# Order of the first stage of a hybrid encoder layer: written order on all engines, earlier scaling of query and key banks, stores from the wide weight tile

## The chip, the cores and the metric

The kernel runs on one core of a Trainium2 chip. The metric is the device time of one execution in microseconds (us); lower is better. Three runs of the kernel before gave 2736.58, 2729.5 and 2735.8 us, median 2735.8 us. One further execution was profiled; all rows below come from it.

## The reference

One layer on a sequence of 2048 tokens of width 1024, cut to what matters:

```python
mod = silu(c) @ w_ada + b_ada                     # six vectors: shift, scale, gate, twice
h = rmsnorm(x, g_norm1) * (1 + sc1) + sh1
q_sb, k_sb, v_sb, q_ca, k_ca, v_ca = split(h @ w_in)
o_sb = stick_breaking_attention(q_sb, k_sb, v_sb) # 8 heads
q_ca, k_ca = rmsnorm(q_ca, g_q), rmsnorm(k_ca, g_k)   # per head of 64
o_ca = chunked_relpos_attention(q_ca, k_ca, v_ca, rel_bias)  # 8 heads
x = x + gt1 * (concat(o_sb, o_ca) @ w_o)
x = x + gt2 * (relu(h2 @ w1) ** 2 @ w2)           # h2: the second norm of x
```

The matrices are fp32. The kernel splits each operand into a high and a low part (`split`: ScalarE copies the high part, a subtraction gives the low one) and multiplies three times, high by high, high by low and low by high (`mm3`). Every product is thus three matmuls.

## The kernel before, in words

The kernel has three stages: the input projection (this change), the two attentions with their output projection, and the MLP. Only the first stage is touched.

**Tiles and jobs.** The sequence has four blocks of 512 tokens, numbered 3 to 0. Weights come in pieces: pieces 0 to 3 are halves of the query and key columns of the first head group (256 columns each, 1 MB raw), 4 and 10 are the values of the two groups, 6 and 8 the queries and keys of the second group (512 columns, two raw tiles of 1 MB). A job is (f, piece, block). A small piece gives two PSUM banks, a large one four; a bank is 8 steps of `mm3`, 24 matmuls. The first three pieces (2, 0, 1) of block 3 are multiplied together while the data arrive; their weights are split into one tile `wide` (pieces 0 and 1) and four tiles of the weight pool (piece 2). Then the list `jobs` runs: 58 banks up to the last job and 4 more in the last one, 62 in all.

**Pools.** A raw weight tile comes from a ring of three (`load_raws`), a split weight from a pool of nine (`weight_parts`, two rows of 512 fp32 each). A split weight that the later stage needs is stored to scratch memory `scr_w`; its buffer is free for the next piece when TensorE has read it and the store has landed. `wide` and the normalised blocks 2 and 0 share one buffer (tag `hp`). PSUM has six banks for this stage, used in turn. Staged results (`st`, `sv`, `wow`) share three buffers.

**Second group.** For pieces 6 and 8 each bank of raw queries or keys needs a norm per head: ScalarE squares it (`csq`), VectorE reduces it (`cv`), GpSimd takes the inverse root in five small operations (`cy`), VectorE scales the bank into `qh` (`scale`). After the fourth bank TensorE transposes the four `qh` into `px` banks (`turn`), two at a time, which are then scaled, split and stored. `later` holds `scale` and `turn` back by a number of banks (a tick follows each bank): 2 for `scale`, 3 and 4 for the two halves of `turn`.

**Block norms.** `start_norm` squares and sums the eight tiles of a block, `norm_rstd` and `norm_spread` (banks `pva` and `pra`) make the inverse root and spread it, VectorE multiplies the tiles by it, and `end_norm` scales, shifts and splits them into the block's `ht`, eight tiles one after the other on ScalarE and VectorE. `hook` says at which bank this happens.

**Side work.** `ada` loads a row group of `w_ada` and, two ticks later, takes a dot product of it on VectorE (`CUSTOM_DVE_ANT_0`, printed as ISA in the order). `prepare_bias` and `prepare_wo` bring the bias and the output weights into scratch memory. A credit per bank in `run_job` paces them.

**Order.** `Ordered` wraps an engine so that its instructions keep the order in which the program is written. TensorE has this throughout. The other engines and the DMA queue of SyncE have it for the first three pieces and from job 7 on; for the jobs ahead of it (`n < ORDERED`) a list scheduler chose their order. In either case the order is fixed when the kernel is built, and each engine takes its list strictly in turn.

Of the kernel before, what the change touches and what calls it, by code (L numbers as in the profile page):

```python
# [18 lines left out]
P = 128  # L19
# [6 lines left out]
TB = 512  # L26
# [53 lines left out]
def encoder_kernel(ctx, tc, xT, c, g1, g2, w_in, w_rest, gqk, bias, w_o, w1, w2, w_ada, b_ada, out):  # L80
# [161 lines left out]
    if True:  # L242
# [48 lines left out]

        def weight_parts(key, m):

            f, p = key
            w = w_tile(f"{f}_{p}_{m}")
            wts.setdefault(key, []).append(w)
            if p < 4:
                src = raws[key, 0][:, 2 * m : 2 * m + 2, :]
                hi, lo = (w[:, l, :].rearrange("p (k c) -> p k c", c=CW) for l in range(2))
# [15 lines left out]

        def weight_of(key, k):
            if key[1] < 4:
                w = wts[key][k // 2]
                return [w[:, l, (k % 2) * CW : (k % 2 + 1) * CW] for l in range(2)]
            return wts[key][k][:, 0, :], wts[key][k][:, 1, :]  # L320
# [6 lines left out]

        staged = {}

        def half_tile(nm, n):  # L330

            if n % 2 == 0:
                staged[0] = stp.tile([P, 2, 2, TB], F32R, tag="st", name=f"st{nm}")
            return staged[0][:, n % 2]

        def project(key, tb, ht, last):
# [3 lines left out]
            if piece < 4:  # L340
                kind, hf = divmod(piece, 2)
                for n in range(2):
# [10 lines left out]
                    store_qk(kind, 0, ps, half_tile(f"{nm}_{n}", n), hf * 2 + n, tb)  # L353
# [4 lines left out]
            for tt in range(4):  # L358
# [4 lines left out]
                for k in range(KT):  # L363
                    mm3(ps, ht[k][:, 0, tl], ht[k][:, 1, tl], *weight_of(key, k), k == 0, k == KT - 1)
                    if last and tt == 3:
                        free[0] += 1
                        pump()
                if kind == 2:
# [28 lines left out]
                later.add(2, scale)  # L397
                if tt == 3:
                    def turn(n):
# [3 lines left out]
                        store_qk(kind, 1, pt, half_tile(f"{nm}_{n}", n), n, tb, gqk_s[:, kind : kind + 1])  # L403

                    for n in range(4):
                        later.add(3 + n // 2, lambda n=n: turn(n))
# [24 lines left out]
        xts, hts = {}, {}  # L431

# [72 lines left out]
        w2s = [w_tile(f"first_{m}").rearrange("p l (k c) -> p l k c", c=CW) for m in range(4)]  # L505
        pss = [pp.tile([P, TB], F32, tag="ps", name=f"pq{p}_3_{n}") for p in first for n in range(2)]

        def first_w(k):
            wr = wraw[k // 2][:, k % 2]
            split(wide[:, k, 0, :, :], wide[:, k, 1, :, :], wr[:, 0:2, :], pool)  # L510
            split(w2s[k // 2][:, 0, k % 2], w2s[k // 2][:, 1, k % 2], wr[:, 2, :], pool)
# [10 lines left out]
        for k in range(KT):  # L522
# [10 lines left out]
            if k + 4 < KT:  # L533
                first_x(k + 4)
            for m, p in enumerate(first):
                hi, lo = [w2s[k // 2][:, l, k % 2] if p == 2 else wide[:, k, l, p] for l in range(2)]
# [6 lines left out]
        act, dve, pool = nc.scalar, nc.vector, nc.gpsimd  # L543
        osp.dma_start(gcol[:, 1, :], g2)
        osp.dma_start(gqk_sb, gqk)
        dve.tensor_scalar_mul(gqk_s[:, 0:1], gqk_sb[:, 0:1], 0.125)
        dve.tensor_copy(gqk_s[:, 1:2], gqk_sb[:, 1:2])
        jobs = [(0, 3, 3), (0, 6, 3), (0, 6, 2), (2, 3, 2), (2, 2, 2), (2, 0, 2), (2, 1, 2)]
        jobs += [(0, p, t) for p in (8, 4, 10) for t in (3, 2)]
        jobs += [(1, p, t) for p, t in ((6, 1), (6, 0), (8, 1), (8, 0), (4, 1))]  # L550
        keys = list(dict.fromkeys((f, p) for f, p, _ in jobs))
        loads = [(key, m) for key in keys for m in range(1 if key[1] < 4 else 2)]
        count = {key: 4 if key[1] < 4 else KT for key in keys}

        def load_raws(*q):

            while loads and len(raws) - sum(len(wts.get(k, ())) >= (4 if k[1] < 4 else 4 * m + 4) for k, m in raws) < 3:
                load_raw(*loads.pop(0), *q)

        free[0] += 4  # L560
        load_raw(*loads.pop(0), osp)
        load_x(2, osp)
        load_raws(osp)
        for m in range(4):
            weight_parts((0, 3), m)
        for m, p in enumerate(first):
            for n in range(2):
                grp, hf = divmod(p, 2)
                store_qk(grp, 0, pss[2 * m + n], half_tile(f"f{p}_3_{n}", n), hf * 2 + n, 3)
# [6 lines left out]
        ORDERED = 7  # L576
        start_norm(2, 2, 2)

        def hook(job, n):

            if (job, n) == ((0, 6, 3), 2):
                norms.flush()
                end_norm(2, h_tile(2))
                load_x(1)
# [13 lines left out]
        def run_job(n):  # L598
            nonlocal credit, act, dve, pool, sp
# [10 lines left out]
            for b in range(2 if key[1] < 4 else 4):  # L610
# [5 lines left out]
                credit += 2.2 if n >= ORDERED else 3.0 * (key[1] in CAQK)  # L616
# [1037 lines left out]
```

## Time and profile before

| | |
|---|---|
| median of three runs | 2735.8 us |
| profiled execution | 2737.15 us |
| its span on the profiler's clock | 2735.4 us |
| first stage: start to the first score matmul `z` | 0 to 462.67 us |
| TensorE busy over the span | 96% |
| mean granted TensorE clock | 0.984 |

The profiled execution is 1.75 us longer than its span and 1.35 us above the median. In rows of a timeline the columns are start and length in us, engine, line, operation, out<-in and count; in brackets stands the idle time of the engine just before and what ended it. L42 is the line of the wrapper `Ordered`; rows with L147, L215 and the like are from the jobs that the scheduler ordered. Rows of waits give us in total, how often, and the longest. `PEclk` is the granted TensorE clock as a share of full speed.

### The profile page before, as it was taken

To read this page: it belongs to the slowest core of one execution; us is meant where nothing else is said; L and a number is where in the kernel's file an instruction comes from. 1 tells how busy PE (TensorE), PEld (TensorE's weight loads), DVE (VectorE), ACT (ScalarE), POOL (GpSimd) and SP (SyncE) were. 2 spreads that over 40 slices of the span, in tenths; PEclk is the share of its full clock that TensorE was granted. 3 is DMA by queue.
4 is the path that set the end of the run, shared out by engine and by line. 5 is a ranking of instruction groups with operands and counts; after the bars stand their busy time and mean duration, and the time that the engine had idled before them with its cause. 6 is when DMAs were issued, how large, how long until landed. Compare 5 with 4: busy or idle time off the path is not lost. (4 is left out here: it accounts for less than half of the span.)

```text
span 2735.4 us, 40253 instructions
## 1 busy us (share of the span) xinstructions
PE 2622.0 (96%) x12944; PEld 2175.4 (80%) x12944; DVE 1922.0 (70%) x3215; ACT 1527.2 (56%) x2966; POOL 997.4 (36%) x1244
## 2 busy tenths in 40 slices
PE   7989999899899999999998999999999999999999
PEld 5767777778778988878776788878888888888887
DVE  7625664788789988989856778877866656655565
ACT  6423443788678877878653444455644444544443
POOL 4422043566456656767533332302101232300000
PEclk9999999999999999999999999999999999999999
DMA  9697967878888688766776777796665434365574
GB/s 341 240 351 277 338 271 238 254 247 249 268 252 263 201 243 266 231 207 190 214 247 224 248 264 260 252 333 228 235 245 201 153 140 162 140 237 199 202 261 155
DMA packets 265333, 651.28 MB, mean 238 GB/s; under 512 B 29856, under 2 KB 65696, under 8 KB 254240
## 3 DMA queue, kind: packets, MB, share of 16 engines
q1 hardware_dynamic: 264336, 646.60, 69.4%
q10 hardware_dynamic: 784, 2.10, 0.3%
q8 instruction: 103, 1.69, 0.3%
q14 instruction: 110, 0.90, 0.1%
HBM read 457.21 MB, written 191.37 MB: 237 GB/s over the span
## 5 line engine op out<-in xcount | busy, mean ns | idle before, releaser
L42 PE MATMUL ps<-h,opw 128*128 128x512 f32 x2664 | 609.8, 391 | 6.3 <-DVE cx L42 6.0
L42 PE MATMUL ps<-oph,opv 128*128 128x512 f32 x2688 | 610.9, 390 | 0.0
L42 PEld LDWEIGHTS ps<-h,opw 128*128 128x128 f32 x2664 | 500.6, 188 | 114.9 <-DVE cx L42 9.1
L42 PEld LDWEIGHTS ps<-oph,opv 128*128 128x128 f32 x2688 | 504.8, 188 | 104.5
L42 POOL TENSOR_TENSOR b<-b,p 128x512 f32<-128x512 f32 (+1 forms) x320 | 359.7, 1124 | 198.8 <-DVE p L42 176.3
L42 DVE TENSOR_TENSOR wtl<-wt,wth 128x512 fp32r<-128x512 f32 (+3 forms) x544 | 290.3, 545 | 50.4 <-ACT wth L42 47.9
L42 ACT CAST wth<-wt 128x512 fp32r<-128x512 f32 (+3 forms) x544 | 257.5, 484 | 119.7 <-PE wt L42 104.4
L42 PE MATMUL pt<-w,ht 128*128 128x512 f32 x1248 | 301.0, 402 | 19.3 <-ACT w L147 8.1
L42 DVE TENSOR_TENSOR oph<-hw,oph 128x512 fp32r<-128x512 f32 x224 | 161.0, 719 | 212.6 <-ACT oph L42 212.6
L42 ACT CAST oph<-hw 128x512 fp32r<-128x512 f32 x224 | 139.3, 622 | 288.9 <-PE ps L42 271.1
L42 PEld LDWEIGHTS pt<-w,ht 128*128 128x128 f32 x1248 | 239.1, 193 | 73.7 <-issue 10.9
L42 DVE TENSOR_TENSOR_SCAN p<-z,p,zero 128x512 f32<-128x512 f32 x192 | 246.0, 1281 | 34.4 <-ACT z L42 28.9
L42 POOL TENSOR_TENSOR ts<-w 128x512 f32<-128x512 f32 x32 | 44.6, 1394 | 549.6 <-DMA w<-in_w_dram 492.5
L42 PE MATMUL acc<-wth,v 128*128 128x512 f32 (+3 forms) x544 | 223.2, 414 | 1.4 <-DMA v<-scr_v 1.4
L42 ACT ACTIVATE b<-z 128x512 f32<-128x512 f32 (+1 forms) x320 | 171.4, 536 | 64.1 <-PE z L42 47.3
L42 POOL TENSOR_TENSOR e<-e,cols 128x640 f32<-128x640 f32 (+4 forms) x128 | 142.9, 1120 | 148.0 <-DVE cols L42 84.5
L42 PE MATMUL z<-k,q 128*128 128x512 f32 (+3 forms) x640 | 186.2, 373 | 9.0 <-DVE p L42 7.0
L42 PE MATMUL acc<-wtl,v 128*128 128x512 f32 (+3 forms) x544 | 187.3, 351 | 0.0
L42 PE MATMUL wt<-ident,b 128*128 128x128 f32 x1088 | 173.3, 275 | 7.0 <-DVE cols L42 5.0
L42 DVE TENSOR_TENSOR opw<-w,opw 128x512 fp32r<-128x512 f32 x127 | 96.9, 764 | 116.4 <-ACT opw L42 116.3
L42 PE MATMUL po<-fx,ow 128*128 128x512 f32 x576 | 167.4, 406 | 4.7 <-DMA ow<-scr_wo 4.7
L42 ACT ACTIVATE z<-z 128x512 f32<-128x512 f32 (+1 forms) x320 | 170.6, 533 | 0.0
(223 smaller groups left out, 4330.5 us busy)
## 6 DMA issues: line engine op xcount, KB each, us to landing
hw<-scr_hid SPq DMA_DIRECT2D x112, 512.0 KB, 3.8
v<-scr_v SPq DMA_DIRECT2D x136, 256.0 KB, 3.8
k<-scr_k SPq DMA_DIRECT2D x268, 128.0 KB, 4.0
w<-in_w_dram SPq DMA_DIRECT2D x64, 512.0 KB, 5.1
hw<-scr_s SPq DMA_DIRECT2D x64, 512.0 KB, 4.6
q<-scr_q SPq DMA_DIRECT2D x124, 256.0 KB, 5.1
fw<-scr_w SPq DMA_DIRECT2D x28, 1024.0 KB, 6.7
wa<-in_w_ada_dram SPq DMA_DIRECT2D x48, 512.0 KB, 7.1
```

The costliest lines, as they stand in the source:

```text
L42: return lambda *x, **y: self.tc.keep_in_program_order(f(*x, **y))
```

## The change

Seven edits, all in the first stage:

1. All engines and the DMA queue keep written order throughout; the switch at job 7 is gone.
2. `scale` of a bank goes right behind the next bank's matmuls (`scale_last`), one tick earlier, and `turn` comes after 2 and 3 ticks in place of 3 and 4.
3. In `jobs`, piece 8 moves ahead of pieces 0 and 1 of block 2; piece 8 stood behind them.
4. Pieces 0 and 1 are stored to `scr_w` from `wide`, in two DMAs of 2 MB, at the second bank of the first job; only pieces 2 and 3 are stored from weight tiles. Those have a new layout (high and low side by side), so a store of one tile is one DMA of 512 KB in place of two of 256 KB.
5. The low parts of the small pieces are subtracted on VectorE, not on GpSimd.
6. Loads: the first raw weight and block 2 are asked for inside the loop of the first three pieces; block 1 and block 0 one bank later; the second gains `gcol` and `gqk` behind the first stores, and the two small operations on `gqk` one job later.
7. `start_norm` of block 0 waits 3 ticks for its second part in place of 2; the credit per bank is 1.9 for large pieces, 2.0 or 1.0 (times f) for small ones, in place of 3.0, 0 or 2.2.

```diff
-            split(hi, lo, src, pool if p < 4 else dve)
-            if f == 2:
-                for l, x in enumerate((hi, lo)):
-                    behind.add(2, lambda l=l, x=x: sp.dma_start(scr_w[p,][:, 2 * m : 2 * m + 2, l, :], x.bitcast(F32)))
+            split(hi, lo, src)
+            if f == 2 and p > 1:
+                behind.add(2, lambda: sp.dma_start(scr_w[p,][:, 2 * m : 2 * m + 2], four(w).bitcast(F32)))
...
+        def scale_last():
+            while scales:
+                scales.pop(0)()
...
+                scale_last()
...
-                later.add(2, scale)
+                scales.append(scale)
...
-                        later.add(3 + n // 2, lambda n=n: turn(n))
+                        later.add(2 + n // 2, lambda n=n: turn(n))
...
+        jobs = [(0, 3, 3), (0, 6, 3), (0, 6, 2), (2, 3, 2), (2, 2, 2), (0, 8, 3), (0, 8, 2), (2, 0, 2), (2, 1, 2)]
+        jobs += [(0, p, t) for p in (4, 10) for t in (3, 2)]
...
-        jobs = [(0, 3, 3), (0, 6, 3), (0, 6, 2), (2, 3, 2), (2, 2, 2), (2, 0, 2), (2, 1, 2)]
-        jobs += [(0, p, t) for p in (8, 4, 10) for t in (3, 2)]
...
+            if k == KT - 3:
+                load_raw(*loads.pop(0), osp)
+                load_x(2, osp)
+            if k == KT - 1:
+                for m in range(4):
+                    weight_parts((0, 3), m)
...
-        act, dve, pool = nc.scalar, nc.vector, nc.gpsimd
...
+            if (job, n) == ((0, 3, 3), 1):
+                dve.tensor_scalar_mul(gqk_s[:, 0:1], gqk_sb[:, 0:1], 0.125)
+                dve.tensor_copy(gqk_s[:, 1:2], gqk_sb[:, 1:2])
+                for p in range(2):
+                    sp.dma_start(scr_w[p,], wide[:, :, :, p, :].bitcast(F32))
...
+            if (job, n) == ((0, 10, 2), 1):
                 load_x(0)
-                behind.add(3, lambda: start_norm(0, 2, 1))
+                behind.add(2, lambda: start_norm(0, 3, 1))
...
-            if n == ORDERED:
-                act, dve, pool = (Ordered(tc, e) for e in (nc.scalar, nc.vector, nc.gpsimd))
-                sp = osp
...
-                credit += 2.2 if n >= ORDERED else 3.0 * (key[1] in CAQK)
+                credit += 1.9 if key[1] > 3 else 1.0 * key[0]
```

Three places show what moves. The first is TensorE at the transposes of the first group of queries (`px_6_3_0`, made of the four scaled banks `qh_6_3_0` to `qh_6_3_3` of job (0, 6, 3)). Before, they follow the second bank of the next job, `pt_6_2_1`:

```order
L42 MATMUL pt_6_2_1_1123<-w_6_6_811,ht_949 128x512 x3
L42 MATMUL pt_6_2_1_1123<-w_6_7_820,ht_949 128x512 x3
L42 MATMUL px_6_3_0_1163<-ident,qh_6_3_0_943 128x128
L42 MATMUL px_6_3_0_1163<-ident,qh_6_3_1_1029 128x128
L42 MATMUL px_6_3_0_1163<-ident,qh_6_3_2_1073 128x128
L42 MATMUL px_6_3_0_1163<-ident,qh_6_3_3_1117 128x128
```

With the change they follow its first bank, `pt_6_2_0`:

```order
L42 MATMUL pt_6_2_0_1058<-w_6_6_813,ht_949 128x512 x3
L42 MATMUL pt_6_2_0_1058<-w_6_7_822,ht_949 128x512 x3
L42 MATMUL px_6_3_0_1098<-ident,qh_6_3_0_920 128x128
L42 MATMUL px_6_3_0_1098<-ident,qh_6_3_1_999 128x128
L42 MATMUL px_6_3_0_1098<-ident,qh_6_3_2_1042 128x128
L42 MATMUL px_6_3_0_1098<-ident,qh_6_3_3_1083 128x128
```

They stand one bank of 24 matmuls earlier, and so they do for each of the eight groups of transposes.

The second place is VectorE at the same group, from the last low part of block 2 (`ht` from `xt_7`) to the last scaled bank. Before, the two reductions `cv` stand together and the two scalings together:

```order
L148 TENSOR_TENSOR ht_949<-xt_7_687,ht_949 128x512
L383 TENSOR_REDUCE cv_6_3_2_1017<-csq_6_3_2_1015 128x8
L392 TENSOR_TENSOR qh_6_3_1_1029<-pt_6_3_1_893,cy_6_3_1_923 128x512
L384 TENSOR_SCALAR cv_6_3_2_1017<-cv_6_3_2_1017 128x8
L383 TENSOR_REDUCE cv_6_3_3_1062<-csq_6_3_3_1060 128x8
L260 ISA wa_947,mod<-wa_947,cs,bcol 128x1024
L260 ISA mod 128x1
L384 TENSOR_SCALAR cv_6_3_3_1062<-cv_6_3_3_1062 128x8
L392 TENSOR_TENSOR qh_6_3_2_1073<-pt_6_3_2_990,cy_6_3_2_1020 128x512
L392 TENSOR_TENSOR qh_6_3_3_1117<-pt_6_3_3_1035,cy_6_3_3_1065 128x512
```

With the change each reduction waits behind the scaling of the bank before it, and two dot products (ISA) stand between:

```order
L42 TENSOR_TENSOR ht_949<-xt_7_620,ht_949 128x512
L42 TENSOR_TENSOR qh_6_3_1_999<-pt_6_3_1_895,cy_6_3_1_927 128x512
L42 TENSOR_REDUCE cv_6_3_2_1003<-csq_6_3_2_1001 128x8
L42 TENSOR_SCALAR cv_6_3_2_1003<-cv_6_3_2_1003 128x8
L42 ISA wa_891,mod<-wa_891,cs,bcol 128x1024
L42 ISA mod 128x1
L42 ISA wa_893,mod<-wa_893,cs,bcol 128x1024
L42 ISA mod 128x1
L42 TENSOR_TENSOR qh_6_3_2_1042<-pt_6_3_2_974,cy_6_3_2_1006 128x512
L42 TENSOR_REDUCE cv_6_3_3_1046<-csq_6_3_3_1044 128x8
L42 TENSOR_SCALAR cv_6_3_3_1046<-cv_6_3_3_1046 128x8
L42 TENSOR_TENSOR qh_6_3_3_1083<-pt_6_3_3_1017,cy_6_3_3_1049 128x512
```

The reduction of the fourth bank has moved behind the scaling of the third.

The third place is the DMA queue of SyncE at the last stored weight piece ahead of piece 8. Before, that is piece 1 (`scr_w_221`), whose eight stores of 256 KB stand between stores of queries:

```order
L215 DMA scr_q_2_2_86<-st_1_2_0_1608 128x1024
L306 DMA scr_w_221<-w_1_0_1542 128x2x256 x2
L306 DMA scr_w_221<-w_1_1_1545 128x2x256 x2
L306 DMA scr_w_221<-w_1_2_1548 128x2x256 x2
L306 DMA scr_w_221<-w_1_3_1551 128x2x256 x2
L215 DMA scr_q_2_3_87<-st_1_2_0_1608 128x1024
```

With the change it is piece 2 (`scr_w_222`), four stores of 512 KB behind loads and stores of the two jobs ahead:

```order
L42 DMA scr_k_2_3_119<-st_3_2_0_1320 128x2x512
L42 DMA scr_q_2_2_102<-st_6_2_2_1396 128x1024
L42 DMA scr_q_2_3_103<-st_6_2_2_1396 128x1024
L42 DMA wa_1408<-in_w_ada_dram 128x1024
L42 DMA wr_0_1410<-in_w_in_dram 128x2048
L42 DMA scr_k_2_0_116<-st_2_2_0_1437 128x2x512
L42 DMA scr_w_222<-w_2_0_1351 128x1024
L42 DMA scr_w_222<-w_2_1_1354 128x1024
L42 DMA scr_w_222<-w_2_2_1357 128x1024
L42 DMA scr_w_222<-w_2_3_1360 128x1024
```

The stores of pieces 0 and 1 no longer stand here; those of piece 2 are now the last that piece 8 waits for.

More of the change, by code (lines that the diff above doesn't have):

```diff
@@ L298, in weight_parts @@
                 src = raws[key, 0][:, 2 * m : 2 * m + 2, :]
-                hi, lo = (w[:, l, :].rearrange("p (k c) -> p k c", c=CW) for l in range(2))
+                hi, lo = (four(w)[:, :, l, :] for l in range(2))
             else:
@@ L431, in encoder_kernel, with load_raws @@
         xts, hts = {}, {}
+        jobs = [(0, 3, 3), (0, 6, 3), (0, 6, 2), (2, 3, 2), (2, 2, 2), (0, 8, 3), (0, 8, 2), (2, 0, 2), (2, 1, 2)]
+        jobs += [(0, p, t) for p in (4, 10) for t in (3, 2)]
+        jobs += [(1, p, t) for p, t in ((6, 1), (6, 0), (8, 1), (8, 0), (4, 1))]
+        keys = list(dict.fromkeys((f, p) for f, p, _ in jobs))
+        loads = [(key, m) for key in keys for m in range(1 if key[1] < 4 else 2)]
+        count = {key: 4 if key[1] < 4 else KT for key in keys}
+        def load_raws(*q):
+            while loads and len(raws) - sum(len(wts.get(k, ())) >= (4 if k[1] < 4 else 4 * m + 4) for k, m in raws) < 3:
+                load_raw(*loads.pop(0), *q)
         def load_x(tb, q=None):
@@ L542, in encoder_kernel @@
                     )
-        act, dve, pool = nc.scalar, nc.vector, nc.gpsimd
[L544 to L547, printed above, removed]
-        jobs = [(0, 3, 3), (0, 6, 3), (0, 6, 2), (2, 3, 2), (2, 2, 2), (2, 0, 2), (2, 1, 2)]
-        jobs += [(0, p, t) for p in (8, 4, 10) for t in (3, 2)]
[L550 to L558, printed above, removed]
-        free[0] += 4
[L561 to L565, printed above, removed]
+        free[0] += 4
+        sp = osp
+        load_raws()
         for m, p in enumerate(first):
@@ L583, in hook @@
                 end_norm(2, h_tile(2))
+            if (job, n) == ((0, 6, 2), 1):
                 load_x(1)
```

28 lines of the change are left out of this document (16 added, 12 removed).

## The prediction

> **What bounds the kernel now.** The page comes first, with the busy times and the largest group of the first stage:
>
> ```profile
> PE 2622.0 (96%) x12944; PEld 2175.4 (80%) x12944; DVE 1922.0 (70%) x3215; ACT 1527.2 (56%) x2966; POOL 997.4 (36%) x1244
> L42 PE MATMUL pt<-w,ht 128*128 128x512 f32 x1248 | 301.0, 402 | 19.3 <-ACT w L147 8.1
> ```
>
> TensorE is the bound, and the change adds and removes no matmul. So only TensorE's idle time in the first stage can change. The second row confirms the count of banks: 1248 matmuls are 52 banks of 24; with the ten banks of small pieces that makes 62. The waits of TensorE up to 520 us name what holds it (total, times, longest):
>
> ```profile
> PE pva L42 <- DVE nsaa L42: 17.7, 2, 12.5
> PE pt L42 <- ACT w L147: 8.1, 3, 7.1
> PE pt L42 <- DVE qh L42: 7.3, 2, 4.6
> PE pt L42 <- DVE qh L392: 2.9, 1, 2.9
> ```
>
> The 12.5 us is the kernel's start, already in written order and not touched. The others lie behind 59.79 us. TensorE's timeline shows where, and what follows each:
>
> ```profile
> 59.79 11.04 PE L42 MATMUL pq<-ht,w 128*128 128x512 f32 x48
> 83.33 22.05 PE L42 MATMUL pt<-w,ht 128*128 128x512 f32 x96
> 105.22 1.03 PE L42 MATMUL px<-ident,qh 128*128 128x128 f32 x8
> 106.01 5.71 PE L42 MATMUL pt<-w,ht 128*128 128x512 f32 x24
> 115.49 7.30 PE L42 MATMUL pt<-w,ht 128*128 128x512 f32 x24 [2.90 <-DVE qh L392]
> 140.64 17.94 PE L42 MATMUL pq<-ht,w 128*128 128x512 f32 x78
> 186.14 32.54 PE L42 MATMUL pt<-w,ht 128*128 128x512 f32 x129 [7.08 <-ACT w L147]
> 218.52 1.03 PE L42 MATMUL px<-ident,qh 128*128 128x128 f32 x8
> 228.63 18.20 PE L42 MATMUL pt<-w,ht 128*128 128x512 f32 x72 [2.74 <-DVE qh L42]
> 332.10 1.84 PE L42 MATMUL pva<-ones,nsaa 128*128 128x1 f32 x8 [5.20 <-DVE nsaa L42]
> 382.80 18.34 PE L42 MATMUL pt<-w,ht 128*128 128x512 f32 x72 [4.59 <-DVE qh L42]
> 462.67 0.61 PE L42 MATMUL z<-k,q 128*128 128x512 f32 x2
> ```
>
> Undisturbed, four banks take 105.22 - 83.33 = 21.89 us, 5.47 each, and a pair of transposed banks 106.01 - 105.22 = 0.79. From 59.79 to 462.67 lie 402.9 us. Work in them: 62 x 5.47 = 339.1, 16 pairs x 0.79 = 12.6, and six small norm steps that I put at 0.8 each, 4.9: together 356.6. So **46.3 us are lost**, and that is all the change can win behind 59.79 us. Of these, 140.64 to 218.52 loses most: 77.9 us for 11 banks (5 small ones and 6 of piece 8), 60.2 us of work, 17.7 lost.
>
> A wait costs more than itself. After the 2.90 us the next bank takes 7.30 in place of 5.71, 1.6 more, and the windows show why (the third number from the right is the granted share of the clock, behind it DMA share and GB/s):
>
> ```profile
> 115.00:120.00 5.00, 4.51 (x13) 3.59 (x14) 2.33 (x5) 2.01 (x4) 3.17 (x4) 0.68 1.00 339
> 145.00:150.00 5.00, 5.00 (x23) 4.14 (x23) 1.41 (x2) 2.02 (x4) 2.72 (x3) 1.00 1.10 404
> 150.00:155.00 5.00, 5.00 (x23) 4.13 (x22) 0.69 (x1) 0.59 (x1) 0.00 (x0) 1.00 0.89 274
> 70.00:71.00 1.00, 1.00 (x8) 0.88 (x6) 0.84 (x3) 0.80 (x3) 0.00 (x0) 1.00 0.37 148
> ```
>
> The granted clock is 0.68 in the stretch behind that wait. I add 1.6 us to each wait above 2 us. The Trainium skill (TensorE: Matmul & The Clock Gate, What's actually happening) says that the clock halves only after an idle window of about 3.4 us. Here a wait of 2.90 us already did it, so the row decides; by the page the one wait of 2.3 us below would be 0.8 us cheaper.
>
> **What goes.** The waits for `qh` at 115.49, 228.63 and 382.80 are waits for a PSUM bank: `scale` stood two ticks back, so a bank was held until after the next but one was due. With the scale one bank earlier its buffer is free in time: `qh` ends some 5.1 us behind its bank (below), and with two pairs of transposes between, its buffer is needed 0.79 + 5.47 + 0.79 = 7.1 us behind. The 5.20 us for `pva` go because that sum gets one more bank (5.47) of cover. The losses between 140.64 and 218.52 are waits for weight buffers whose stores had not landed; pieces 0 and 1 have no such stores any more. If every loss went, the time would be 2737.15 - 46.3 = 2690.9. But each earlier or reordered step meets a new limit.
>
> **What is late next: the transposes.** The chain from the end of a bank to its `qh`, at a quiet place:
>
> ```profile
> 413.85 0.60 ACT L42 ACTIVATE csq<-pt 128x512 f32<-128x512 f32 x1 [4.58 <-PE pt L42]
> ```
>
> ```profile
> 414.48 0.69 DVE L42 TENSOR_REDUCE cv<-csq 128x8 f32<-128x512 f32 x1 [3.49 <-ACT csq L42]
> 97.88 1.27 DVE L260 CUSTOM_DVE_ANT_0 wa<-wa,cs,bcol 128x1024 f32<-128x1024 f32 x1
> 223.81 0.68 DVE L42 TENSOR_TENSOR qh<-pt,cy 128x512 f32<-128x512 f32 x1
> ```
>
> ```profile
> 415.45 1.64 POOL L42 TENSOR_TENSOR cy<-cv,mhalf 128x8 f32<-128x8 f32 x1 [3.50 <-DVE cv L42]
> 418.01 0.20 POOL L42 TENSOR_TENSOR cy<-cy,ct 128x8 f32<-128x8 f32 x1
> ```
>
> From 413.85 the inverse root is ready at 418.21, 4.36 later; with 0.68 for `qh`, 5.1 us. The transposes now start one bank, 5.47 us, behind the fourth bank. It fits by 0.4 us where nothing else is in the way. For six of the eight groups I count 0.3 each for jitter, **2 us** (bounds 0, and 4.6 each in the rival below).
>
> Two groups have something in the way: jobs (0, 6, 3) and (1, 6, 1), where the norm of the next block is applied between. The start of it, and its pace in written order:
>
> ```profile
> 82.51 1.06 PE L42 MATMUL pra<-ndga,ones 128*128 128x128 f32 x8
> ```
>
> ```profile
> 84.66 1.52 ACT L199 ACTIVATE xt<-xt,mod,aff 128x512 f32<-128x512 f32 x2 [1.35 <-DVE xt L450]
> 305.67 0.81 ACT L42 ACTIVATE xt<-xt,mod,aff 128x512 f32<-128x512 f32 x1
> 307.04 0.81 ACT L42 ACTIVATE xt<-xt,mod,aff 128x512 f32<-128x512 f32 x1
> ```
>
> Each of eight tiles takes 307.04 - 305.67 = 1.37 us on ScalarE. From 84.66 that is 95.6; the last low part on VectorE ends at 96.3, the second bank's `qh` at 96.9, the third's reduction and small step at 97.7. Its root is done 2.8 us later, 100.5 (the two dot products of 1.27 fit beside it), its `qh` at 101.1, then the fourth's reduction to 101.9, its root to 104.7, its `qh` to 105.4. TensorE is through the three banks behind `pra` at 83.33 + 3 x 5.47 = 99.7. It waits 5.7 us at the fourth transpose, and 1.6 more for the clock: 7.3. Before, the transposes came at 105.22 and hid all of this. Behind `pra` of block 0 the same chain runs with the same distances: again 7.3. **14.6 us** for both. They could be less by the 0.69 of one VectorE step each, and cannot vanish while the order of the rows stands.
>
> **The weights of piece 8.** Its last three tiles need the buffers of piece 2, so the four stores of 512 KB must land. Count from t, the end of the first bank of job (2, 3, 2). From t + 1.9 the queue gets, by the order: a store of keys, four of piece 3, two of queries, a bias and a row group (4.5 MB), then keys, two queries, a row group and a raw weight (3.1 MB). At 0.395 MB/us (the 404 GB/s of the window 145 to 150, a little lower) that is 19.3 us. Then keys and the first store of piece 2, 1.05 MB, 2.7, and 1.5 for the receipt, which I estimate: t + 25.4. Split, 1.4: t + 26.8. TensorE comes to that tile at t + 3 x 5.47 + 2 x 0.79 + 5 x 0.69 = t + 21.4. It waits 5.4, and 1.3 more at the next two tiles, since stores follow at 1.33 and matmuls at 0.69. With the clock 8.3, I take **8 us**. The bounds: the store group's own row and the wait it caused before,
>
> ```profile
> scr_w<-w SPq DMA_DIRECT2D x64, 256.0 KB, 6.2
> ```
>
> ```profile
> 185.47 0.62 ACT L147 CAST w<-wr 128x512 fp32r<-128x512 f32 x1 [7.92 <-DMA scr_w<-w]
> ```
>
> 6.2 us to landing from an issue at t + 14.4 gives a wait of 0.7; the other end is the 17.7 of before. The value is near the middle, from bytes counted.
>
> **The weights behind block 0's norm.** Without the wait for `pva`, TensorE comes earlier to the weights of (1, 6, 1), whose split stands behind eight squares on ScalarE:
>
> ```profile
> 329.60 0.63 ACT L42 ACTIVATE nsqa<-xt 128x512 f32<-128x512 f32 x1 [0.17 <-DVE nsaa L42]
> 330.40 0.63 ACT L42 ACTIVATE nsqa<-xt 128x512 f32<-128x512 f32 x1 [0.17 <-DVE nsaa L42]
> 331.87 4.25 ACT L42 CAST w<-wr 128x512 fp32r<-128x512 f32 x8
> ```
>
> The squares run at 0.8 us each behind VectorE. They start 0.6 behind the end of bank 2; three at 0.6 and five at 0.8 end at 6.4, the first weight's copy at 7.0, its low part at 7.8. TensorE comes at 5.47: 2.3, with half the clock's price **3 us** (0 to 5.2, the wait it replaces).
>
> **Small terms.** `gqk` now loads behind six stores of 512 KB; the queue runs dry at about 70.5 (148 GB/s in 70 to 71), so VectorE, which waits for it in order, gets to the weights of (0, 6, 3) near 72 and TensorE, due at 71.5, loses **1 us** (0 to 3). The stores from `wide` hold the buffer of block 2: 0.5 + 4.2 MB behind 70.5 at 0.40 end at 82.3, 84 with receipt; ScalarE first writes there at 85.4, and TensorE would not notice before 87.9. At the 274 GB/s of the window 150 to 155 they would land at 89.2: 0 taken, 1.3 at most. The low parts on VectorE, the fewer issues and the credit cost nothing: 59.79 has no wait ahead of it, and the dot products are as many.
>
> **Sum.** 2 + 14.6 + 8 + 3 + 1 = 28.6 us of new or remaining loss against 46.3. The profiled execution's 2737.15 - 17.7 = **2719.5 us**. The median of the runs shown is 1.35 lower, within the spread of the runs.
>
> **The rivals.** First, the queue has room and no weight waits: 8 becomes 0.7 and 3 becomes 0, 2719.5 - 10.3 = 2709. For it speaks the landing time of 6.2, against it the DMA share of 1.10 in 145 to 150. Second, the other way: the chain of 5.1 us does not fit in the bank's 5.47 at the six other groups either. The place is the dot product on VectorE ahead of a reduction or a scaling. One, 1.27 late, makes each group wait 1.3, with the clock 2.9: 6 x 2.9 - 2 = 15 more, 2735. Two, and GpSimd late by 0.5, make it 4.6 each: 26 more, **2745, slower**. It decides from 4.4 us a group. For it speaks how thin 0.4 us is; against it, that GpSimd's 2.8 us usually cover one dot product. That the change would not move the scaling is excluded by the order: `qh` of a bank stands ahead of the next bank's reduction.
>
> **How the numbers follow.** Forecast, 2710 to 2727: 0.50. No weight waits, or better: 0.20. One dot product late at each group, about 2735: 0.16. Two, about 2745: 0.14. A measurement of this kernel tells about 0.3% from no change, 8.2 us: faster is under 2727.6, slower over 2744.0. So faster 0.70, same 0.16, slower 0.14. The range takes in the forecast, most of the first rival and both sizes of the second: 2700 to 2746.
>
> **What would show it.** In the new profile: no wait of `pt` for `qh`; waits of `px` for `qh` of 5 to 6 us near 100 us and once more in (1, 6, 1); a wait of `pt` for `w` at the first bank of piece 8 behind `scr_w`; the first `z` at about 445 us. Wrong would be: `px` waiting at all eight groups, a wait for `ht` behind `wide`, or a changed length behind the first `z`.

## The result, and the profile after

The changed kernel takes 2731.8 us (median of 12 runs), the kernel before 2736.2 us in the same session (12 runs): the ratio is 0.9984, with a 95% interval of 0.9973 to 0.9996. It is faster, by 4.4 us where 17.7 were forecast; that is less than the 8.2 us (0.3%) from which the forecast would have called a kernel faster, so by its own measure this is "same", which it gave a chance of 0.16. The profiled execution took 2732.43 us with a span of 2730.6; the first score matmul `z` starts at 455.71 us, 6.96 earlier than before and not the 17.7 that would put it at 445.

First the page of the changed kernel, its engines and the largest group of the stage (columns as in the same rows of before):

```profile
PE 2615.5 (96%) x12944; PEld 2169.4 (79%) x12944; DVE 1934.3 (71%) x3235; ACT 1525.4 (56%) x2966; POOL 972.9 (36%) x1224
...
L42 PE MATMUL pt<-w,ht 128*128 128x512 f32 x1248 | 297.6, 399 | 12.5 <-ACT w L42 11.9
```

TensorE is as busy as before and the bound as before. What it waits for up to 560 us has changed (total, times, longest):

```profile
PE px L42 <- DVE qh L42: 12.6, 6, 4.0
PE pva L42 <- DVE nsaa L42: 11.9, 1, 11.9
PE pt L42 <- ACT w L42: 11.9, 2, 6.2
PE pra L42 <- DVE ndga L42: 4.3, 2, 3.3
```

All waits of `pt` for `qh` are gone (they were 10.2 us), and so is the second wait for `nsaa`; only the one at the kernel's start is left. In their place transposes (`px`) wait for `qh`, and the waits of `pt` for weights have grown from 8.1 to 11.9 us, in two places. TensorE's timeline of the changed kernel shows the places:

```profile
59.97 11.04 PE L42 MATMUL pq<-ht,w 128*128 128x512 f32 x48
...
102.68 0.33 PE L42 MATMUL px<-ident,qh 128*128 128x128 f32 x1 [1.92 <-DVE qh L42]
107.04 1.33 PE L42 MATMUL px<-ident,qh 128*128 128x128 f32 x5 [4.03 <-DVE qh L42]
108.02 7.00 PE L42 MATMUL pt<-w,ht 128*128 128x512 f32 x24
...
159.55 26.95 PE L42 MATMUL pt<-w,ht 128*128 128x512 f32 x105 [5.70 <-ACT w L42]
...
323.38 0.80 PE L42 MATMUL pt<-w,ht 128*128 128x512 f32 x1 [6.20 <-ACT w L42]
...
339.60 1.13 PE L42 MATMUL pra<-ndga,ones 128*128 128x128 f32 x8 [1.04 <-DVE ndga L42]
...
362.66 1.33 PE L42 MATMUL px<-ident,qh 128*128 128x128 f32 x5 [4.04 <-DVE qh L42]
...
455.71 0.61 PE L42 MATMUL z<-k,q 128*128 128x512 f32 x2
```

From here on **lost** means what it meant in the prediction: the time from the first full `pq` bank to the first `z`, less 356.6 us of work. Here that is 455.71 - 59.97 - 356.6 = 39.1 us, where 46.3 were lost before and 28.6 were forecast. Cut at the same places, each stretch's elapsed time less its banks (5.47), pairs of transposes (0.79) and norm steps (0.8) gives:

| place | forecast | lost |
|---|---|---|
| transposes behind the norms of blocks 2 and 0 | 14.6 | 8.2 + 7.5 = 15.7 |
| weights of piece 8 behind the stores of piece 2 | 8 | 8.7 |
| weights of (1, 6, 1), then `pra` | 3 | 9.4 + 1.4 = 10.8 |
| `gqk` and the start | 1 | 0.5 |
| the other transposes, and the rest | 2 | 3.4 |
| sum | 28.6 | 39.1 |

Two large terms came out as worked; the third is more than three times its forecast. Behind the first `z` the profiled execution takes 2274.9 us, before 2272.7. In the 14 profiled executions of this study that stretch, whose code is the same in all, lies between 2267.8 and 2276.6 us, so these 2.2 us say nothing, and kernels are compared below by what the stage loses beside their ratio to the kernel before. One run of the kernel half below took 4312.92 us and is left out of its median.

### The profile page after: what moved, and what is told of

Its sections match the earlier page's. It is cut to its first block, busy times and chain, and to the rows that moved or that the text cites. A ratio compares the mean times of both kernels' runs of the same rounds, so it can differ in the third digit from the quotient of the medians.

```text
span 2730.6 us, 40192 instructions
## 1 busy us (share of the span) xinstructions
PE 2615.5 (96%) x12944; PEld 2169.4 (79%) x12944; DVE 1934.3 (71%) x3235; ACT 1525.4 (56%) x2966; POOL 972.9 (36%) x1224
## 3 DMA queue, kind: packets, MB, share of 16 engines
q8 instruction: 103, 1.69, 0.3%
## 5 line engine op out<-in xcount | busy, mean ns | idle before, releaser
L42 PE MATMUL pt<-w,ht 128*128 128x512 f32 x1248 | 297.6, 399 | 12.5 <-ACT w L42 11.9
L42 DVE TENSOR_TENSOR opw<-w,opw 128x512 fp32r<-128x512 f32 x127 | 102.5, 808 | 116.5 <-ACT opw L42 116.3
```

The costliest lines, as they stand in the source:

```text
L42: return lambda *x, **y: self.tc.keep_in_program_order(f(*x, **y))
```

## The experiments

Each is the changed kernel with the edit shown in its section. Lost time and `z` come from one profiled execution. The ratio is to runs of the kernel before in the same session (medians 2736.9 to 2737.4 us beside the experiments); the changed kernel did not run again beside them, so experiments are compared with it through these ratios.

| kernel | lost, us | first `z`, us | median, us | ratio (95% interval) |
|---|---|---|---|---|
| before | 46.3 | 462.67 | 2736.2 | 1 |
| changed | 39.1 | 455.71 | 2731.8 | 0.9984 (0.9973 to 0.9996) |
| turn | 32.4 | 448.45 | 2721.5 | 0.9944 (0.9932 to 0.9956) |
| half | 30.7 | 448.55 | 2724.3 | 0.9955 (0.9940 to 0.9970) |
| store1 | 34.7 | 451.76 | 2726.4 | 0.9965 (0.9952 to 0.9979) |
| wo4 | 42.6 | 459.69 | 2729.8 | 0.9973 (0.9962 to 0.9983) |
| wo4norm0 | 38.6 | 455.72 | 2730.3 | 0.9981 (0.9969 to 0.9993) |
| quiet | 37.7 | 453.89 | 2727.2 | 0.9969 (0.9958 to 0.9980) |
| scale_old | 33.7 | 452.10 | 2725.9 | 0.9959 (0.9944 to 0.9974) |
| jobs_old | 42.6 | 458.83 | 2734.2 | 0.9990 (0.9980 to 1.0001) |
| wide_old | 50.9 | 467.14 | 2739.2 | 1.0008 (0.9996 to 1.0020) |
| undo_234 | 47.2 | 463.21 | 2736.0 | 0.9999 (0.9986 to 1.0013) |
| combo_half | 23.3 | 439.44 | 2710.3 | 0.9899 (0.9878 to 0.9919) |
| combo_turn | 22.8 | 440.82 | 2710.9 | 0.9899 (0.9882 to 0.9917) |

### The transposes behind a block norm: turn and half

VectorE's timeline of the changed kernel around the first group:

```profile
96.97 0.69 DVE L42 TENSOR_TENSOR ht<-xt,ht 128x512 fp32r<-128x512 f32 x1 [0.68 <-ACT ht L42]
97.58 0.68 DVE L42 TENSOR_TENSOR qh<-pt,cy 128x512 f32<-128x512 f32 x1
98.18 0.68 DVE L42 TENSOR_REDUCE cv<-csq 128x8 f32<-128x512 f32 x1
...
102.54 0.67 DVE L42 TENSOR_REDUCE cv<-csq 128x8 f32<-128x512 f32 x1
...
106.29 0.69 DVE L42 TENSOR_TENSOR qh<-pt,cy 128x512 f32<-128x512 f32 x1 [2.87 <-POOL cy L42]
```

The eighth tile of the block ends, then come the second `qh`, the third reduction, and one root later the third `qh`, the fourth reduction and the fourth `qh`, which ends at 107.0 us. The forecast had 105.4; 0.6 of the difference is that `pra` came 0.6 later. Two edits take parts of this away in different ways.

```diff
-                        later.add(2 + n // 2, lambda n=n: turn(n))
+                        held = 3 if (key, tb) in (((0, 6), 3), ((1, 6), 1)) else 2
+                        later.add(held + n // 2, lambda n=n: turn(n))
```

> Only the transposes of the two groups behind a block norm, (0, 6, 3) and (1, 6, 1), go back one bank (3 and 4 ticks); the scaling stays early. My theory: the 8.22 and 7.48 us that TensorE loses there in the changed kernel are waits for the fourth scaled bank, which is ready some 6 us too late; one bank more of cover (5.47 us plus a pair of transposes) hides it, so both losses fall to about 0.5 each and the time to 2731.8 - 14.7 = 2717. The rival: a bank of PSUM is then missing, as before the change, and pt waits for qh at the same two places, 3 to 6 us each; the time stays within 4 us of 2731.8.

TensorE's timeline of that kernel, the two groups:

```profile
105.67 0.76 PE L42 MATMUL px<-ident,qh 128*128 128x128 f32 x5 [0.33 <-DVE qh L42]
...
114.49 3.68 PE L42 MATMUL pt<-w,ht 128*128 128x512 f32 x15 [1.69 <-DVE qh L42]
```

```profile
365.45 6.86 PE L42 MATMUL pt<-w,ht 128*128 128x512 f32 x22 [2.73 <-DVE qh L42]
```

Both were right in part. The waits of `px` fell to 0.33 and none, but a bank of PSUM is then missing, and `pt` waits for it, 1.69 and 2.73 us. With the clock 7.4 us stay lost at the two places in place of 15.7.

```diff
-        def end_norm(tb, ht):
+        def end_norm(tb, ht, ks=range(KT)):
...
-            for k in range(KT):
+            for k in ks:
...
-                end_norm(2, h_tile(2))
+                end_norm(2, h_tile(2), range(4))
+            if (job, n) == ((0, 6, 3), 3):
+                end_norm(2, hts[2], range(4, KT))
...
-                end_norm(0, h_tile(0))
+                end_norm(0, h_tile(0), range(4))
+            if (job, n) == ((1, 6, 1), 3):
+                end_norm(0, hts[0], range(4, KT))
```

> All of the changed kernel, but the eight tiles of a block norm (blocks 2 and 0) are applied in two halves, one bank apart, with the third bank's norm of queries between them. My theory: the fourth scaled bank is late only because all eight tiles stand ahead of the third bank's reduction and scaling on VectorE; with four of them behind, its root is ready near 100.3 and the fourth qh near 101, so the waits of px of 5.95 and 5.01 us fall under 1 each and TensorE's loss in the first stage from 39.1 by some 14 to 25. The first score matmul moves to about 442, the time to 2718. No wait for a PSUM bank takes their place, unlike with the transposes one bank later. The rival: the second half makes ht late for the next job, and pt waits for ht 2 to 5 us at each place.

TensorE's timeline again, the two groups:

```profile
104.13 1.33 PE L42 MATMUL px<-ident,qh 128*128 128x128 f32 x5 [2.38 <-DVE qh L42]
...
355.07 0.77 PE L42 MATMUL px<-ident,qh 128*128 128x128 f32 x5 [1.36 <-DVE qh L42]
```

In halves, the waits of `px` are 2.38 and 1.36 us, where under 1 was expected, and nothing waits for `ht` or a PSUM bank. The stage loses 8.5 us less than the changed kernel, where 14 to 25 were expected. At the two places 5.9 us stay lost, so 9.8 of the 15.7 are shown to be due to the order of rows on VectorE, as the forecast had it; what holds the rest in half was not tried.

### Piece 8: store1

```diff
-                behind.add(2, lambda: sp.dma_start(scr_w[p,][:, 2 * m : 2 * m + 2], four(w).bitcast(F32)))
+                behind.add(1, lambda: sp.dma_start(scr_w[p,][:, 2 * m : 2 * m + 2], four(w).bitcast(F32)))
```

> The stores of pieces 2 and 3 to scr_w are issued one bank earlier, ahead of a row group and a raw weight (pieces 3 and 2) and of two stores of queries (piece 2). My theory: the wait of 5.70 us at the first bank of piece 8 is the place in the queue; 2.5 MB fewer ahead of it are 6.3 us at 0.395 MB/us, so the segment's loss of 8.73 us falls under 1.5 and the time to about 2724. The rival: the queue is full anyway and what is issued later (raw weight of piece 8, a dot product's rows) becomes late in place of it; the loss stays at 6 to 9 us.

In the changed kernel ScalarE sat idle ahead of the weights of piece 8 until a store landed:

```profile
158.88 0.62 ACT L42 CAST w<-wr 128x512 fp32r<-128x512 f32 x1 [10.68 <-DMA scr_w<-w]
```

With the stores one bank earlier TensorE runs through all five banks there without a wait:

```profile
150.95 27.37 PE L42 MATMUL pt<-w,ht 128*128 128x512 f32 x120
178.15 0.49 PE L42 MATMUL px<-ident,qh 128*128 128x128 f32 x3
```

27.20 us from the one to the other are the five banks of 5.47. The 8.7 us were due to the place of these stores in the queue, and the rival falls. Half of it, 4.4 us, reaches the first `z`; TensorE now comes earlier to the transposes at 178 and 380 us, which wait 1.4 and 3.0 us for a `qh`.

### Block 0's weights: wo4, wo4norm0, quiet

This is the term that failed. ScalarE of the changed kernel at the place:

```profile
315.47 1.05 ACT L42 CAST wow<-wo 128x1024 fp32r<-128x1024 f32 x1 [7.48 <-DVE mod L42]
316.43 0.58 ACT L42 CAST sv<-pt 128x512 fp32r<-128x512 f32 x1
316.90 0.63 ACT L42 ACTIVATE nsaa<-xt 128x512 f32<-128x512 f32 x1
```

The squares of block 0 (`nsaa`, `nsqa`) start at 316.9 and not at 312.3, 0.6 behind a bank's end at 311.7. ScalarE stood idle for 7.5 us with the split of an output weight at its head. (The row names the last step of a dot product, which ends at 315.46. But the output weight, which the split reads, lands 9.0 us behind its issue at 306.40, at 315.4.) My first theory was that wait.

```diff
-            behind.add(2, rest)
+            behind.add(4, rest)
```

(In `prepare_wo`.)

> The split of an output weight stands 4 ticks behind its load, not 2. In the changed kernel ScalarE sat 7.5 us ahead of such a split until 315.5 us, with the last values of block 2, the squares of block 0 and the weights of (1, 6, 1) behind it, and TensorE lost 9.40 us there. Theory A, ScalarE's wait for that load is the whole cause: the loss falls to about 3, the time by 6 to about 2725.5. Theory B, the dot product on VectorE at 314.2 us, which also waited for its rows, holds the sums of the squares as long: the loss falls by 2 only, to 2730.

9.4 became 7.8, the size that theory B gave. That proves little: turn, half, store1 and jobs_old, which leave this place as it is, lose 7.8 to 8.8 us there too, scale_old 10.1 and wide_old 12.2. But ScalarE and VectorE of this kernel show a third cause:

```profile
316.70 0.63 ACT L42 ACTIVATE nsaa<-xt 128x512 f32<-128x512 f32 x1 [2.77 <-DMA xt<-in_xT_dram]
```

```profile
314.80 1.28 DVE L42 CUSTOM_DVE_ANT_0 wa<-wa,cs,bcol 128x1024 f32<-128x1024 f32 x1 [2.09 <-DMA wa<-in_w_ada_dram]
```

Without the output weight ahead, the squares wait for block 0 itself. Output weight, rows and block are behind one another in one queue. Theory A falls, and B names a wait that is there but does not hold the first square. The stage as a whole lost 3.5 us more than the changed kernel, at other places to which the splits moved.

```diff
-                behind.add(2, lambda: start_norm(0, 3, 1))
+                behind.add(3, lambda: start_norm(0, 2, 1))
```

(With the edit of wo4.)

> As the run with 4 ticks, and the squares of block 0 start one bank later, behind the splits of the weights of (1, 6, 1) (3 ticks and 2 in place of 2 and 3; pva stays where it is). By both theories the weights then stand behind nothing that waits for the queue: low parts from about 316, TensorE is due at 317.1 and waits under 1 us; the squares end near 323 and pva may wait 1. The losses of 9.40 and 1.41 us fall to 2 together, the time by 8 to 9, to about 2723. Against it: if the raw weights themselves come late, the wait for w stays over 4 us.

```profile
329.32 1.84 PE L42 MATMUL pva<-ones,nsaa 128*128 128x1 f32 x8 [4.48 <-DVE nsaa L42]
```

The weights are in time, but the sums are late: 6.9 us are lost up to the bank behind `pra` in place of 10.8, not the 2 expected. VectorE still stands ahead of its rows for 2.1 us, so the low parts, the output weight and the sums all come later. Changing the order on the engines moved the wait; so the next run took load off the queue.

```diff
-                credit += 1.9 if key[1] > 3 else 1.0 * key[0]
+                quiet = (key[1], t, b) in ((10, 3, 2), (10, 3, 3), (10, 2, 0), (10, 2, 1), (10, 2, 2))
+                credit += 0 if quiet else 1.9 if key[1] > 3 else 1.0 * key[0]
```

> No credit for side work in five banks, from the third of (0, 10, 3) to the third of (0, 10, 2): two loads for dot products, an output weight and their work on ScalarE and VectorE move behind (1, 6, 1); the squares stay where the change put them. My theory: what held the squares of block 0 till 316 to 317 us is the queue, whose 390 GB/s delayed the loads of block 0, of the output weight and of the dot product alike; 1.5 MB less ahead of the loads is 4 us, so the squares start near 313 and TensorE's loss at the weights of (1, 6, 1) and pra falls from 10.8 to 3 to 5, the first score matmul to about 449. The rival: the loads of block 0 wait for their buffers, which the norm of block 1 holds until 308; then the squares start at 316 all the same and the loss stays over 8.

First the DMA queue of the changed kernel, then that of this one, then its ScalarE and TensorE:

```profile
306.40 0.65 SPq L42 DMA_DIRECT2D wo<-in_w_o_dram  x1
307.09 8.70 SPq L42 DMA_DIRECT2D xt<-in_xT_dram  x8
```

```profile
305.00 6.56 SPq L42 DMA_DIRECT2D xt<-in_xT_dram  x8
```

```profile
312.37 0.63 ACT L42 ACTIVATE nsaa<-xt 128x512 f32<-128x512 f32 x1
```

```profile
318.65 0.49 PE L42 MATMUL pt<-w,ht 128*128 128x512 f32 x1 [1.37 <-ACT w L42]
319.68 5.52 PE L42 MATMUL pt<-w,ht 128*128 128x512 f32 x23 [0.53 <-DVE w L42]
325.04 0.95 PE L42 MATMUL pva<-ones,nsaa 128*128 128x1 f32 x8
```

The loads of block 0 are issued 2.1 us earlier and 2.1 us faster, the last at about 311.5 and not 315.8. The first of them lands 7.1 us behind its issue, at 312.1; in the changed kernel it took 9.0 us, to 316.1. The squares start at 312.37, right behind the bank. From 273.48, where nine banks begin, to `pva` are 51.56 us, 49.23 of them work: **2.3 us are lost, the size of the wait that the forecast had worked out** (the rows show 1.37 + 0.53 = 1.9 us of it as waiting), and 1.4 at `pra`. The rival, buffers held until 308, falls. Yet the first `z` came only 1.8 us earlier, since the work moved: at 433.56 a transpose waits 3.53 us for a `qh`, with two dot products ahead of the weights' low parts on VectorE and an output weight's split behind them, none of which stood there in the changed kernel; with the bank behind it that costs 6.3.

### Undoing the parts: scale_old, jobs_old, wide_old, undo_234

```diff
-                scales.append(scale)
+                later.add(2, scale)
...
-                        later.add(2 + n // 2, lambda n=n: turn(n))
+                        later.add(3 + n // 2, lambda n=n: turn(n))
```

> Only the scaling and the transposes go back to where they stood (2, 3 and 4 ticks); all else is as changed. My theory: the two waits behind the block norms (15.7 us) go, and waits of pt for qh, for a PSUM bank, come back at three places as in the kernel before (4.6, 4.8 and 7.4 us with the clock), so the first score matmul stays within 3 us of 455.7: this part of the change by itself is worth nothing. The rival: the early scaling is worth most of the 17 us that I gave it and hides behind the new waits; then the stage is over 8 us longer here.

```profile
118.59 7.73 PE L42 MATMUL pt<-w,ht 128*128 128x512 f32 x21 [4.02 <-DVE qh L42]
```

The waits for a PSUM bank come back at two places (three were expected), 14.0 us with the clock, and the 15.7 go; but the stage is 5.4 us shorter, not within 3. Besides the exchange, piece 8 loses only 5.5 us: the last two stores of queries (1 MB) now stand behind the stores of piece 2 in the queue, which are issued at 146.01 and not at 147.75, while TensorE begins the piece at the same time (150.38 and 150.26). The other transposes lose less too. As built, the earlier scaling and transposes cost 5 us. The rival falls.

```diff
-        jobs = [(0, 3, 3), (0, 6, 3), (0, 6, 2), (2, 3, 2), (2, 2, 2), (0, 8, 3), (0, 8, 2), (2, 0, 2), (2, 1, 2)]
-        jobs += [(0, p, t) for p in (4, 10) for t in (3, 2)]
+        jobs = [(0, 3, 3), (0, 6, 3), (0, 6, 2), (2, 3, 2), (2, 2, 2), (2, 0, 2), (2, 1, 2)]
+        jobs += [(0, p, t) for p in (8, 4, 10) for t in (3, 2)]
```

> Only the order of the jobs goes back: piece 8 behind pieces 0 and 1 of block 2. My theory: piece 8 then reuses the buffers of pieces 0 and 1, which no store holds any more, and the loss of 8.73 us at its first bank goes; pieces 0 and 1 need four buffers each, of which those of piece 2 have two more jobs' time to be stored. The first score matmul moves to about 447.5. The rival: the small pieces, 10.9 us each, come faster than the queue stores; waits for w then show at pieces 0 and 1, 6 to 17 us in all, as in the kernel before.

```profile
165.04 10.21 PE L42 MATMUL pq<-ht,w 128*128 128x512 f32 x30 [4.57 <-ACT w L42]
```

The rival was right: the wait moves to a small piece (7.9 us with the clock, where 8.7 go), and a transpose behind it loses 6.6. The new order of jobs is worth 3.5.

```diff
-            if f == 2 and p > 1:
+            if f == 2:
...
-                for p in range(2):
-                    sp.dma_start(scr_w[p,], wide[:, :, :, p, :].bitcast(F32))
```

> Only the stores of pieces 0 and 1 go back to the weight tiles (one DMA of 512 KB each, two ticks behind the split). My theory: the same bytes, but the eight buffers of pieces 0 and 1 are then held until their stores have landed, and piece 4, which follows, waits for them as piece 8 does for piece 2: 4 to 9 us more lost near the first bank of (0, 4, 3), the first score matmul at 460 to 465. The rival: the queue has room there, or the 4 MB that are gone from 76 to 83 us relieve piece 8 as much, and the stage stays within 3 us.

```profile
237.22 7.96 PE L42 MATMUL pt<-w,ht 128*128 128x512 f32 x24 [5.72 <-ACT w L42]
```

At (0, 4, 3) 8.9 us are lost, within the 4 to 9 expected, and with 2.8 more at block 0's weights 11.7 in all, so that `z` comes at 467.14, behind the 460 to 465 expected. This is the part of the change that pays most.

The last of these runs joins the three edits above.

> Scaling and transposes, the order of the jobs, and the stores of pieces 0 and 1 all go back; what is left of the change is written order from the first job on, the layout of the small weights, the low parts on VectorE, the earlier loads and the credit. My theory: the waits of the kernel before come back, about 17 us for PSUM banks and up to 17 for weight buffers, with the 10.8 at the weights of (1, 6, 1) beside them; some 45 us lost, the first score matmul at about 461, the time that of the kernel before within 0.3%. The rival: written order itself is worth something; then the loss stays under 40.

47.2 us are lost and the time is that of before. So the rest of the change, written order among it, is together worth nothing that can be seen; its parts were not tried one by one. Each by itself, the parts are worth -5.4 (scaling and transposes), 3.5 (jobs) and 11.7 (stores from `wide`) by the stage, 9.8 together; undone at once they cost 8.1. By the ratios the three are -7, 2 and 7 us, each uncertain by about 5, so the signs of the first and the third are shown and that of the second is not.

### Cures together: combo_half and combo_turn

The edits of store1, quiet and half (or turn), and the dot products three ticks behind their loads:

```diff
-            behind.add(2, lambda: ada_column(j, wa))
+            behind.add(3, lambda: ada_column(j, wa))
```

> Four cures at once: the block norms in two halves, the stores of pieces 2 and 3 one bank earlier, the five banks without side work, and dot products three ticks behind their loads in place of two (in the run with halves, VectorE sat 3.5 us ahead of one for its rows, with a qh behind it). My theory: the losses add, since each has its own place. 39.1 less 11 (norms), 7.5 (piece 8), 7 (block 0's weights) and 3 (dot products) leave 10 to 13 us, the first score matmul at about 428, the time near 2703. The rival: what one cure frees is lost at the next full stretch of the queue, as the run without side work lost 6 us again at later transposes; then over 20 us stay lost and the time is 2712 or more.

> As the run before this one, but with the transposes of the two groups behind a block norm one bank later in place of the norms in halves. My theory: waits for a PSUM bank stay at these two places, 1.9 and 4.6 us as with that edit alone, so 2 to 5 us more are lost than with halves: the first score matmul at about 431. The rival: the halves delay ht or the fourth qh more than the bank costs, and this one is as fast or faster.

TensorE's two largest waits of combo_half from 60 to 440 us:

```profile
PE px L42 <- DVE qh L42: 10.8, 6, 2.6
PE pt L42 <- ACT w L42: 1.4, 1, 1.4
```

Both are 1% faster than the kernel before, and the fastest of all. In the stage they lose 16 us less than the changed kernel, where 26 to 29 were expected: over 20 us stay lost, as the rival said, though the time is between the two theories'. (By the ratios, 0.9899 beside 0.9984, the distance is 23 us; for wo4 the two measures differ as much, 3 us faster by the ratio and 3.5 slower by the stage of its one profile. The scatter behind `z` and the intervals leave this much open.) What TensorE waits for now is almost all transposes. At the longest of them (2.58 us) VectorE has done its dot products without a wait, but the eight low parts of the weights, 4.91 us, stand ahead of `qh`:

```profile
360.63 4.91 DVE L42 TENSOR_TENSOR w<-wr,w 128x512 fp32r<-128x512 f32 x8
365.46 0.68 DVE L42 TENSOR_TENSOR qh<-pt,cy 128x512 f32<-128x512 f32 x1
...
369.81 0.69 DVE L42 TENSOR_TENSOR qh<-pt,cy 128x512 f32<-128x512 f32 x1 [2.87 <-POOL cy L42]
```

Dot products three ticks behind their loads did not help this place: the wait for the rows went, but two dot products now stand ahead of the low parts where one stood in half, and the place loses 4.5 us with the clock, where it lost 3.6 in half. Halves and late transposes come out alike (23.3 and 22.8), as the rival had it, so the halves are not the better of the two.

## Why the prediction was wrong in size

- **What goes** was right. No `pt` waits for `qh`, the 5.20 for `pva` are gone, and the stores from `wide` free the buffers of pieces 0 and 1.
- **The transposes behind the norms**, 14.6 forecast, 15.7 measured, at both places and by the rows that the forecast counted, though part of the wait came at the third transpose (1.92 and 0.97 us) and not at the fourth. half and turn show the cause for 9.8 and 8.3 of the 15.7.
- **Piece 8**, 8 forecast, 8.7 measured; store1 shows that it is the place in the queue. The parts agree less well than the sum. The wait is 5.70 for 5.4, no wait came at the next two tiles (1.3 in the forecast), and the rest, 3.0, is the clock, for 1.6: its granted share was 0.50 from 160 to 165 us. No run shows the 1.5 us for the receipt by itself; the first store of piece 2 landed 11.0 us behind its issue, at 158.8, where the forecast's t + 25.4 is 157.5.
- **Block 0's weights** are the step that failed: "They start 0.6 behind the end of bank 2". The working from there on gave 2.3 us, which quiet then lost, but it took the data of block 0 to be there. They were asked for at 307 to 316 us, behind an output weight, rows for dot products and sixteen stores of 256 KB. The first of them landed 9.0 us behind its issue, at 316.1, 4.4 us behind the bank's end at 311.7. So TensorE waited 6.4 us (6.20 + 0.23) where 2.3 were worked out, and the slower clock behind it cost 3.0 where half a price, 0.7, stood: 9.4 in place of 3. The bound of 5.2, taken from another wait, did not hold it. The trace of before had a hint that I passed over. There, too, the first square waited for its load, which had been issued at 314.86 and took 8.5 us (the row is below this list), and without the wait for `pva` TensorE would only come earlier.
- **`pra`** has 1.4 that no term held. It stays in quiet, without dot products ahead. There VectorE waits 4.97 us for GpSimd, which takes the root of a bank of queries ahead of the root of the block, so it is the chain through GpSimd.
- **The price of a wait**, 1.6 us for each above 2 us, came from one wait and did not hold: 3.0 at piece 8 and at block 0's weights, and nothing at some other places (last section).
- **Small terms**: `gqk` 0.5 for 1, no wait for `ht` behind `wide`, the other transposes and the rest 3.4 for 2. The rival that the chain fails at all six other groups did not come; single groups wait 0.2 to 1.5 us. That 2731.8 lies near this rival's 2735 is chance.
- **Sum**: 28.6 forecast, 39.1 lost. 7.8 of the 10.5 between are block 0's weights and `pra`, 1.1 the norms, 0.7 piece 8, and 0.9 net the small terms. With the 2.2 us behind `z`, which scatter, and 0.2 at the start this is the 12.9 between 2719.5 and the profiled 2732.4.

The first square of block 0 in the kernel before, by ScalarE's timeline:

```profile
323.40 0.63 ACT L42 ACTIVATE nsaa<-xt 128x512 f32<-128x512 f32 x1 [1.31 <-DMA xt<-in_xT_dram]
```

One thing was right in the sum and hidden by it: what "goes" by the earlier scaling and what is "late next" behind it nearly cancel, and scale_old shows the part as a loss. A sum by part of the change, beside the one by place, would have said so.

## What to carry to other kernels

When a wait is taken away and an engine arrives earlier, follow the data of everything that stands at the new place back to the issue of its load, and count the bytes ahead in the queue: here a better order on the engines did little while the data themselves came late. An edit that shortens a chain only pays if nothing in written order stands between its links, so look at the rows of the engine that carries it, here a block norm's eight tiles. And price each part of a change by itself, since one that costs can hide behind one that pays.

## What was not expected of the hardware

Whether a short idle time of TensorE lowers its granted clock does not hang on its length alone. In combo_half it waits 2.29 us twice, each time between the third and the fourth transpose, but the bank behind takes 5.71 us once and 7.34 the other time:

```profile
102.68 0.77 PE L42 MATMUL px<-ident,qh 128*128 128x128 f32 x5 [2.29 <-DVE qh L42]
103.20 5.71 PE L42 MATMUL pt<-w,ht 128*128 128x512 f32 x24
...
342.57 0.77 PE L42 MATMUL px<-ident,qh 128*128 128x128 f32 x5 [2.29 <-DVE qh L42]
343.09 7.34 PE L42 MATMUL pt<-w,ht 128*128 128x512 f32 x24
```

The granted share (third number from the right) is 1.00 behind the first and 0.84 behind the second:

```profile
105.00:110.00 5.00, 5.00 (x28) 4.24 (x27) 1.29 (x3) 1.06 (x2) 0.94 (x5) 1.00 0.93 333
345.00:350.00 5.00, 5.00 (x20) 4.02 (x19) 0.76 (x2) 0.00 (x0) 0.82 (x5) 0.84 1.01 380
```

The Trainium skill (TensorE: Matmul & The Clock Gate, What's actually happening) says that the activity is watched in a window of about 3.4 us that runs freely, so that the moment of the idle time matters. These rows agree with that, but not with the length: 2.29 us of idle time already cost 1.6. Nor does the longer wait cost more. At the transposes near 380 us, half waits 3.25 us and the bank behind takes 5.74; turn waits 1.88 us and it takes 6.97, with a granted share of 0.66 from 380 to 385 us where half has 1.00. First half, then turn:

```profile
382.12 0.77 PE L42 MATMUL px<-ident,qh 128*128 128x128 f32 x5 [3.25 <-DVE qh L42]
382.64 5.74 PE L42 MATMUL pt<-w,ht 128*128 128x512 f32 x24
```

```profile
380.42 1.28 PE L42 MATMUL px<-ident,qh 128*128 128x128 f32 x5 [1.88 <-DVE qh L42]
381.35 6.97 PE L42 MATMUL pt<-w,ht 128*128 128x512 f32 x24
```

What decides was not tried. The clock also differs from one execution to the next: in the 22 runs of the kernel before beside combo_half its mean granted share lies between 0.982 and 0.987, and the time falls by about 1.9 us for each 0.001 more (correlation -0.70). So part of the scatter between runs goes with the clock.
